# Nine instead of seven up-projection pairs computed as seven half-size products, arranged two and two with one plain pair between

## The chip, the cores and the metric

The kernel runs on one core of one Trainium2 chip. The metric is the device time of one execution in microseconds (us). Engines are named as in the profile: PE is TensorE's matmul and PEld its weight load, DVE is VectorE, ACT is ScalarE, POOL is GpSimd, SP is the SyncE queue that issues most loads. POOL issues its own DMAs.

## The reference

One layer of an encoder: token mixing, cross-attention into a memory, and a gated MLP, each in RMSNorms with a residual. The change touches the MLP's up-projection alone:

```python
def conv_ffn(h, w_up, conv_w, conv_b, w_down):
    u = h @ w_up                       # (512, 1024) @ (1024, 5632)
    ...
    for j in range(CONV_W):
        acc = acc + up[:, j:j + n] * conv_w[j]
    gate, val = jnp.split(acc, 2, axis=-1)
    return (jax.nn.silu(gate) * val) @ w_down
```

There are 512 tokens, a model width of 1024 and 2816 gate and 2816 value columns, all float32.

## The kernel before

**Precision.** A float32 product is made of three matmuls on operands split in a high part and a low part (`mm3`, L278 to L280): high by high, high by low, low by high. A weight arrives as float32 in a tile called `raw` or `tmp` (128x1024, 512 KB) by a DMA that SP issues (L189). ACT casts it to the high part `wh` (L222). The low part `wl` is made in one of two ways: DVE subtracts (L224), or ACT writes the negated high part into `wl` (L229) and a DMA that POOL issues adds the float32 weight from DRAM onto it (L230, an accumulating DMA). Such a `wh`, `wl` pair is called a unit.

**Units ahead.** Units are consumed in one fixed order (`plan`). `take` and `unit` first issue the work on the unit three places further on (`AHEAD = 3`), and the tile pool `wp` has four buffers each of `wh` and `wl`. So unit n goes into the buffers of unit n-4, and its cast can begin only when PE has read unit n-4 for the last time. Four `raw` rooms (two of pool `rawp`, two of pool `t4`) take the loads, and each pair of up-projection units loads into the rooms of the pair two before it.

**The up-projection.** The 5632 columns are taken as 22 pairs i: 128 gate columns and the 128 value columns that belong to them. A plain pair is two units, `w` and `w'`; each is 8 x 3 matmuls with 512 columns (tokens). A pair listed in `UP_S` goes through `strassen_pair` (L1126 on): token halves and weight quarters, seven products in place of eight, each 4 x 3 matmuls with 256 columns, so 84 matmuls of 256 columns in place of 48 of 512. It has four units:

```python
plan += [(kind, UP_S.index(i)) for kind in ("diag", "side", "sums", "last")]
UP_PRODUCTS = (("w11", 0), ("w22", 1), ("t2", 0), ("w21", 1), ("t3", 1), ("t1", 0), ("t4", 0))
LOW_FROM = {"diag": 0, "side": 512}
```

Unit `diag` serves the first two products, `side` the next two, `sums` two, `last` one. `diag` and `side` are loaded; `sums` and `last` are sums of them that DVE makes (`add_blocks`, L197, L200, L204). By `LOW_FROM`, the low part of the whole of `diag` (512 KB) and of the second half of `side` (256 KB) comes by POOL's accumulating DMA; all other units of this stage use DVE's subtraction:

```python
by_dma = 0 if i in NEG_SCALAR or i in NEG_POOL else LOW_FROM.get(kind, raw.shape[1])
nc.scalar.copy(wh, raw)
if by_dma:
    last_low[0] = nc.vector.tensor_sub(wl[:, :by_dma], raw[:, :by_dma], wh[:, :by_dma].bitcast(F32)).ins
if by_dma < raw.shape[1]:
    ...
        nc.scalar.mul(wl[:, by_dma:], wh[:, by_dma:].bitcast(F32), -1.0)
    nc.gpsimd.dma_start(wl[:, by_dma:], source(i)[:, by_dma:], accum_op=ALU.add)
```

After a pair, `conv` (ACT L1067, DVE L1068 and L1070) filters its two results; ACT's Silu (L1073) and DVE's product (L1081) finish it. In `strassen_pair` ACT copies the first product out of PSUM (L1142) and DVE combines the others (L1144 to L1153). A scheduler orders the instructions on each engine.

**Other work of the stage.** The down-projection after it also uses sums of weight blocks. They are made in DRAM by 24 accumulating DMAs of POOL (L251), which are hung on certain units: POOL first copies a mark from that unit's `wl` (L236), so it waits for DVE, and then issues the DMA. `adds_at` lists those units.

Before, pairs 6, 8, 10, 12, 14, 16 and 18 go through `strassen_pair`; between every two of them lies a plain pair. In the profile they begin at 534.0, 555.1, 576.0, 597.0, 618.0, 639.0 and 659.9 us.

Of the kernel before, what the change touches and what calls it, by code (L numbers as in the profile page):

```python
# [25 lines left out]
FF = 2816  # L26
NF = FF // P
EPS = 1e-6
UP_S = (6, 8, 10, 12, 14, 16, 18)
N_MIX, N_WHOLE = 66, 110 - 2 * len(UP_S)  # L30
N_DOWN = N_WHOLE + 4 * len(UP_S)
N_UNITS = N_DOWN + 42
# [57 lines left out]
def layer(tc, io, out):  # L90
# [54 lines left out]
    plan = [("w", i) for i in range(N_MIX)]  # L145
    whole, adds_at = N_MIX, set(ADDS_AT)
    for i in range(NF):
        if i in UP_S:
            plan += [(kind, UP_S.index(i)) for kind in ("diag", "side", "sums", "last")]
        else:  # L150
            if i >= 2:
                adds_at.update((len(plan), len(plan) + (i - 1 not in UP_S)))
            plan += [("w", whole), ("w", whole + 1)]
            whole += 2
    assert len(plan) == N_DOWN and whole == N_WHOLE
# [970 lines left out]
    def strassen_pair(i):  # L1126
        g, m, n = next_bank(), next_bank(), next_bank()
        place = {"w11": (g, near), "t2": (m, far), "t1": (m, near), "w22": (n, near), "t3": (n, far),
                 "w21": (g, near), "t4": (g, far)}
        two, more, val = tmp2(tag="th"), tmp2(tag="th"), tmp2(tag="tq")  # L1130
        for k, (name, at_w) in enumerate(UP_PRODUCTS):
            if k % 2 == 0:
                w = take()
            (hi, lo), cols = left_h[name]
            o, at = place[name]
            o = o[:, at]
            for kc in range(4):
                wc = slice(at_w * 512 + kc * P, at_w * 512 + kc * P + P)
                mm3(o, (w[0][:, wc], w[1][:, wc]), (hi[:, kc, cols], lo[:, kc, cols]), kc == 0 and name != "w21",
                    kc == 3, name == "w21")  # L1140
            if name == "w11":
                nc.scalar.copy(two[:, near], o)  # L1142
            elif name == "t2":
                nc.vector.tensor_sub(two[:, far], o, two[:, near])  # L1144
            elif name == "t3":
                nc.vector.tensor_add(more[:, far], o, two[:, far])
            elif name == "t1":
                nc.vector.tensor_add(more[:, near], o, two[:, far])
                nc.vector.tensor_tensor(out=val.rearrange("p (a t) -> p a t", a=2),
                                        in0=n.rearrange("p (a t) -> p a t", a=2),  # L1150
                                        in1=more[:, None, near].to_broadcast([P, 2, 256]), op=ALU.add)
            elif name == "t4":
                nc.vector.tensor_sub(o, o, more[:, far])  # L1153
        conv(0, i, g)
        conv(1, i, val)

    for i in range(2, NF):
        if i in UP_S:
            strassen_pair(i)
# [185 lines left out]
```

## Time and profile before

| | |
|---|---|
| median of 3 runs | 816.55 us (816.46 to 817.71) |
| profiled execution, its own time | 816.97 us |
| its span, first to last instruction | 814.8 us |
| granted TensorE clock | 0.999 of full speed |
| PE busy | 804.2 us (99%) |
| DVE, ACT, POOL busy | 574.4, 483.6, 137.2 us |

The time lies 2.2 us above the span, for what comes ahead of the first and behind the last instruction. A busy time is the union of an engine's instructions; matmuls overlap one another, so PE's rate is read from the distance between starts and not from the duration of one. A DMA's time is from its issue to its landing.

### The profile page before, as it was taken

How to read it: one execution, taken by the hardware profiler on the slowest of the kernel's cores; microseconds unless marked ns; L12 is line 12 of the kernel's file. 1: busy time of each engine (PE TensorE's matmuls, PEld its weight loads, DVE VectorE, ACT ScalarE, POOL GpSimd, SP SyncE). 2: the span in 40 equal slices, each digit the busy share in tenths (PEclk: the TensorE clock that was granted, in tenths of full speed). 3: DMA queues.
4: the chain of work that ended last, by engine and by line, in shares of the span. 5: the costliest groups of instructions: out<-in, count | busy, mean ns of one | idle time of the engine just before them, and what ended most of it. 6: DMA issues, size and time to landing. Idle time of an engine off the chain costs nothing.

```text
span 814.8 us, 11771 instructions
## 1 busy us (share of the span) xinstructions
PE 804.2 (99%) x4426; PEld 691.4 (85%) x4426; DVE 574.4 (70%) x866; ACT 483.6 (59%) x798; POOL 137.2 (17%) x213
## 2 busy tenths in 40 slices
PE   9999999999999999999999999999999999999996
PEld 7888888889898887888888898899999998888885
DVE  5456587469886875855453767987777788888765
ACT  5675757469988874645553543665555545566651
POOL 0111201053233101301010311211111101000301
PEclk9999999999999999999999999999999999999999
DMA  8585745569889743256734058676666677278852
GB/s 296 197 262 139 160 104 116 119 161 244 230 237 261 186 162 135 78 181 156 181 117 142 27 167 205 154 197 172 177 168 140 162 193 180 90 209 273 243 128 103
DMA packets 42457, 139.61 MB, mean 171 GB/s; under 512 B 5280, under 2 KB 6560, under 8 KB 42400
## 3 DMA queue, kind: packets, MB, share of 16 engines
q1 hardware_dynamic: 28944, 97.43, 35.2%
q0 software_dynamic: 12160, 38.54, 26.3%
q10 hardware_dynamic: 1296, 2.89, 1.0%
q8 instruction: 34, 0.56, 0.3%
q14 instruction: 23, 0.19, 0.1%
HBM read 135.17 MB, written 25.17 MB: 197 GB/s over the span
## 4 chain that ended last, share of the span: by engine, by line
PE 93%; DVE 3%; ACT 1%; POOL 1%; issue 1%; POOLq 0%; DVEq 0%
PE ps_b L279 10%; PE ps_b L278 10%; PE ps_b L280 10%; PE ps_s L280 6%; PE ps_s L279 6%; PE ps_s L278 6%; PE ps_o L278 5%; PE ps_o L279 5%; PE ps_o L280 5%; PE ps_c L280 5%; PE ps_c L279 5%; PE ps_c L278 5%; PE ps_c L646 3%; PE ps_o L891 2%; PE ps_s L870 2%; PE ps_o L880 2%
## 5 line engine op out<-in xcount | busy, mean ns | idle before, releaser
L222 ACT CAST wh<-raw 128x1024 fp32r<-128x1024 f32 x110 | 113.8, 1036 | 114.8 <-PE ps_b L279 35.7
L224 DVE TENSOR_TENSOR wl<-raw,wh 128x1024 fp32r<-128x1024 f32 (+1 forms) x77 | 92.3, 1200 | 72.1 <-ACT wh L222 72.1
L278 PE MATMUL ps_b<-big,wh 128*128 128x512 f32 (+1 forms) x344 | 122.2, 355 | 0.0
L280 PE MATMUL ps_b<-big,wl 128*128 128x512 f32 (+1 forms) x344 | 121.1, 352 | 0.0
L279 PE MATMUL ps_b<-big,wh 128*128 128x512 f32 (+1 forms) x344 | 120.8, 351 | 0.0
L279 PEld LDWEIGHTS ps_b<-big,wh 128*128 128x128 f32 x344 | 65.1, 189 | 8.3
L280 PEld LDWEIGHTS ps_b<-big,wl 128*128 128x128 f32 x344 | 65.0, 189 | 8.3
L278 PEld LDWEIGHTS ps_b<-big,wh 128*128 128x128 f32 x344 | 65.1, 189 | 8.1
L672 DVE TENSOR_TENSOR big<-big 128x512 f32<-128x512 f32 x64 | 47.5, 755 | 10.6 <-PE ps_c L646 4.2
L278 PE MATMUL ps_s<-wh,big 128*128 128x512 f32 (+1 forms) x140 | 53.4, 382 | 0.0
L279 PE MATMUL ps_s<-wl,big 128*128 128x512 f32 (+1 forms) x140 | 53.3, 381 | 0.0
L280 PE MATMUL ps_s<-wh,big 128*128 128x512 f32 (+1 forms) x140 | 52.9, 378 | 0.0
L230 POOL DMA_DIRECT2D wl<-in_w_dram x33 | 29.4, 890 | 127.9 <-ACT wl L229 87.0
L122 DVE TENSOR_TENSOR big<-ps_o,big 128x512 fp32r<-128x512 f32 x54 | 36.9, 687 | 15.1 <-ACT big L121 13.5
L121 ACT CAST big<-ps_o 128x512 fp32r<-128x512 f32 x54 | 31.8, 589 | 18.5 <-PE ps_o L994 7.5
L278 PE MATMUL ps_s<-big,wh 128*128 128x256 f32 (+1 forms) x120 | 40.0, 333 | 0.0
L279 PE MATMUL ps_s<-big,wh 128*128 128x256 f32 (+1 forms) x120 | 39.9, 333 | 0.0
L280 PE MATMUL ps_s<-big,wl 128*128 128x256 f32 (+1 forms) x120 | 39.9, 332 | 0.0
L278 PE MATMUL ps_o<-wh,big 128*128 128x512 f32 (+1 forms) x102 | 39.2, 384 | 0.0
L279 PE MATMUL ps_c<-big,wh 128*128 128x256 f32 (+1 forms) x120 | 39.1, 326 | 0.0
L278 PE MATMUL ps_c<-big,wh 128*128 128x256 f32 (+1 forms) x120 | 39.0, 325 | 0.0
L280 PE MATMUL ps_c<-big,wl 128*128 128x256 f32 (+1 forms) x120 | 39.0, 325 | 0.0
(313 smaller groups left out, 2150.3 us busy)
## 6 DMA issues: line engine op xcount, KB each, us to landing
raw<-in_w_dram SPq DMA_DIRECT2D x91, 512.0 KB, 3.5
wl<-in_w_dram POOLq DMA_DIRECT2D x33, 512.0 KB, 7.1
sum_t<-in_wd_dram SPq DMA_DIRECT2D x20, 512.0 KB, 6.3
tmp<-in_wu_dram SPq DMA_DIRECT2D x14, 512.0 KB, 6.8
sum_t<-in_wd_dram POOLq DMA_DIRECT2D x10, 512.0 KB, 8.2
sum_t<-sum_t POOLq DMA_DIRECT2D x10, 512.0 KB, 7.8
big<-sum_t SPq DMA_DIRECT2D x10, 512.0 KB, 5.1
raw<-sum_t SPq DMA_DIRECT2D x10, 512.0 KB, 3.8
```

The source lines that it names most:

```text
L121: nc.scalar.copy(hi, src)
L122: (eng or nc.vector).tensor_sub(lo, src, hi.bitcast(F32))
L222: nc.scalar.copy(wh, raw)
L224: last_low[0] = nc.vector.tensor_sub(wl[:, :by_dma], raw[:, :by_dma], wh[:, :by_dma].bitcast(F32)).ins
L230: nc.gpsimd.dma_start(wl[:, by_dma:], source(i)[:, by_dma:], accum_op=ALU.add)
L278: nc.tensor.matmul(o, a[0], b[0], start=start, stop=False, skip_group_check=again)
L279: nc.tensor.matmul(o, a[0], b[1], start=False, stop=False, skip_group_check=again)
L280: last_mm[0] = nc.tensor.matmul(o, a[1], b[0], start=False, stop=stop, skip_group_check=again).ins
L646: nc.tensor.matmul(o[:, b, :], kc[:, blk(b)], qc[:, blk(b)] if m == 1 else pat(qk, b * P, [[2 * m, P // (2 * m)], [T + m, 2], [1, m]]), st ...
L672: nc.vector.tensor_tensor(out=c, in0=c, in1=pat(tt, toff + off, [[2, npair], [gap, 2], [0, m]]), op=ALU.mult)
L870: nc.tensor.matmul(s, qT[h // 4][:, h % 4, blk(qb)], kT[:, 2 * (h // 4) + c, :], start=c == 0, stop=c == 1)
L880: nc.tensor.transpose(o[:, c, :], e[:, 0, blk(c)], ident)
```

## The change

Pairs 6, 8, 9, 11, 12, 14, 15, 17 and 18 go through `strassen_pair`; plain pairs in the stage's middle are 7, 10, 13 and 16. So pairs 9, 12, 15 and 18 follow another such pair directly. The second line changes which plain pairs carry one of POOL's additions and which two: now one where both neighbours are in `UP_S` (7, 10, 13, 16), two elsewhere.

```diff
-UP_S = (6, 8, 10, 12, 14, 16, 18)
+UP_S = (6, 8, 9, 11, 12, 14, 15, 17, 18)
...
             if i >= 2:
-                adds_at.update((len(plan), len(plan) + (i - 1 not in UP_S)))
+                adds_at.update((len(plan), len(plan) + (i - 1 not in UP_S or i + 1 not in UP_S)))
```

**ACT, pair 8.** The rows begin with the last filter of pair 7 and the copy of pair 8's first product. In the rows before, the two raw casts are plain pair 9's units and the `tmp` casts pair 10's `diag` and `side`:

```order
L1067 ACTIVATE tmp_5291<-ps_b,cw 128x512
L1142 COPY tmp_5299<-ps_s 128x256
L222 CAST wh<-raw 128x1024 x2
L222 CAST wh<-tmp_5265 128x1024
L229 ACTIVATE wl<-wh 128x1024
L222 CAST wh<-tmp_5306 128x1024
L1067 ACTIVATE tmp_5418<-ps_s,cw 128x512
L1067 ACTIVATE tmp_5423<-tmp_5301,cw 128x512
L229 ACTIVATE wl<-wh 128x512
```

With the change, the raw casts are pair 9's `diag` and `side`, then come its `sums` and `last`:

```order
L1067 ACTIVATE tmp_5289<-ps_b,cw 128x512
L1142 COPY tmp_5297<-ps_s 128x256
L222 CAST wh<-raw 128x1024
L229 ACTIVATE wl<-wh 128x1024
L222 CAST wh<-raw 128x1024
L229 ACTIVATE wl<-wh 128x512
L222 CAST wh<-both 128x1024
L222 CAST wh<-tmp_5370 128x512
L1067 ACTIVATE tmp_5420<-ps_s,cw 128x512
L1067 ACTIVATE tmp_5425<-tmp_5299,cw 128x512
L1142 COPY tmp_5435<-ps_b 128x256
```

The `diag` that is to follow pair 8 directly is cast in the place where a plain unit was cast, which is the first cast after pair 8's start; before, two plain units came ahead of the next `diag`.

**POOL, pairs 8 to 10.** L230 with 128x1024 is a `diag`, with 128x512 the half of a `side`. Before, one such couple is followed by the mark and the addition that hang on a plain unit (plain pair 9):

```order
L230 DMA wl<-in_wu_dram 128x1024
L230 DMA wl<-in_wu_dram 128x512
L236 COPY mark<-wl 128x1
L251 DMA sum_t_3_3028<-sum_t_3_1976 128x1024
L230 DMA wl<-in_wu_dram 128x1024
L230 DMA wl<-in_wu_dram 128x512
```

With the change, two couples (pairs 8 and 9) come behind one another, and the mark (plain pair 10) after both:

```order
L230 DMA wl<-in_wu_dram 128x1024
L230 DMA wl<-in_wu_dram 128x512
L230 DMA wl<-in_wu_dram 128x1024
L230 DMA wl<-in_wu_dram 128x512
L236 COPY mark<-wl 128x1
L251 DMA sum_t_3_3028<-sum_t_3_1976 128x1024
```

Pair 9's two accumulating DMAs have nothing but pair 8's ahead of them in POOL's order.

## Rows read from the trace of the kernel before

**Rows 1.** The page: busy time of each engine, share of the span, instructions.
```profile
PE 804.2 (99%) x4426; PEld 691.4 (85%) x4426; DVE 574.4 (70%) x866; ACT 483.6 (59%) x798; POOL 137.2 (17%) x213
```

**Rows 2.** PE in order of time around pair 16, and where pair 18 begins and ends.
```profile
638.97 0.28 PE L278 MATMUL ps_s<-big,wh 128*128 128x256 f32 x1
...
639.20 0.28 PE L280 MATMUL ps_s<-big,wl 128*128 128x256 f32 x1
...
649.04 0.40 PE L278 MATMUL ps_b<-big,wh 128*128 128x512 f32 x1
...
659.94 0.28 PE L278 MATMUL ps_c<-big,wh 128*128 128x256 f32 x1
...
670.02 0.40 PE L278 MATMUL ps_s<-big,wh 128*128 128x512 f32 x1
```

**Rows 3.** Windows: pairs 16 and 17, pair 17 alone, pair 16 alone (length, engines, clock, DMA).
```profile
638.97:659.94 20.97, 20.97 (x133) 19.08 (x132) 16.17 (x23) 11.71 (x16) 2.75 (x4) 1.00 0.66 164
649.04:659.94 10.90, 10.90 (x50) 9.01 (x49) 8.58 (x13) 6.68 (x10) 1.73 (x2) 1.00 0.93 233
638.97:649.04 10.07, 10.07 (x86) 10.07 (x85) 7.59 (x11) 5.02 (x7) 1.02 (x2) 1.00 0.36 88
```

**Rows 4.** ACT in order of time during pairs 16 and 17 (start, duration, what).
```profile
641.92 1.05 ACT L222 CAST wh<-raw 128x1024 fp32r<-128x1024 f32 x1 [0.95 <-PE ps_o L279]
644.80 1.05 ACT L222 CAST wh<-raw 128x1024 fp32r<-128x1024 f32 x1 [1.83 <-PE ps_s L279]
647.68 1.05 ACT L222 CAST wh<-tmp 128x1024 fp32r<-128x1024 f32 x1 [1.83 <-PE ps_c L279]
648.80 1.06 ACT L229 ACTIVATE wl<-wh 128x1024 fp32r<-128x1024 f32 x1
...
652.09 0.62 ACT L229 ACTIVATE wl<-wh 128x512 fp32r<-128x512 f32 x1
```

**Rows 5.** POOL in order of time: the issues of pair 18's two accumulating DMAs.
```profile
650.16 0.88 POOL L230 DMA_DIRECT2D wl<-in_wu_dram  x1 [4.54 <-ACT wl L229]
653.00 0.85 POOL L230 DMA_DIRECT2D wl<-in_wu_dram  x1 [1.96 <-ACT wl L229]
```

**Rows 6.** DMA issues in windows at 650.0, 545.0 and 653.0 us: size, time to landing.
```profile
wl<-in_wu_dram POOLq DMA_DIRECT2D x1, 512.0 KB, 8.9
...
wl<-in_wu_dram POOLq DMA_DIRECT2D x1, 512.0 KB, 9.8
...
wl<-in_wu_dram POOLq DMA_DIRECT2D x1, 256.0 KB, 8.0
```

**Rows 7.** PE and POOL in order of time, DMA issue at 531.0 us: pair 6's `side`.
```profile
538.55 0.36 PE L280 MATMUL ps_b<-big,wl 128*128 128x256 f32 x1
538.75 0.28 PE L278 MATMUL ps_b<-big,wh 128*128 128x256 f32 x1
...
531.10 0.88 POOL L230 DMA_DIRECT2D wl<-in_wu_dram  x1 [4.34 <-ACT wl L229]
...
wl<-in_wu_dram POOLq DMA_DIRECT2D x1, 256.0 KB, 7.4
```

**Rows 8.** Mixing stage: SP and POOL issues; DMA at 71.5, 156.5, 164.0 us.
```profile
70.61 0.33 SPq L189 DMA_DIRECT2D raw<-in_w_dram  x1
...
71.97 0.87 POOL L230 DMA_DIRECT2D wl<-in_w_dram  x1 [9.86 <-PE ps_s L280]
...
wl<-in_w_dram POOLq DMA_DIRECT2D x1, 512.0 KB, 5.3
...
wl<-in_w_dram POOLq DMA_DIRECT2D x1, 512.0 KB, 5.2
...
wl<-in_w_dram POOLq DMA_DIRECT2D x1, 512.0 KB, 5.6
```

**Rows 9.** DMA issue at 193.0 us, with two transfers issued within 1.8 us ahead.
```profile
wl<-in_w_dram POOLq DMA_DIRECT2D x1, 512.0 KB, 6.1
```

**Rows 10.** DVE in order of time: the subtraction for one plain unit in this stage.
```profile
622.02 1.23 DVE L224 TENSOR_TENSOR wl<-raw,wh 128x1024 fp32r<-128x1024 f32 x1 [0.46 <-ACT wh L222]
```

## The prediction

> **What bounds the kernel now.** I read the page first. PE is busy 99% of the span [rows 1]. So time is gained only where PE gets less to do, and anything that makes PE wait is lost in full. Then PE in order of time in the stage that changes [rows 2]: pair 16 begins at 638.97 us, pair 17 at 649.04, pair 18 at 659.94 and pair 19 at 670.02. A pair in seven products takes 10.07 or 10.08 us, a plain one 10.90. The windows over the same stretches [rows 3] show PE without a gap, at the full one of its two clock levels (1.00, 2.4 GHz). They show one thing more: DMA is busy 36% while pair 16 runs and 93% while pair 17 runs. The reader is to keep that in mind, since the change moves a DMA from the full stretch into the empty one, but also brings its deadline nearer.
>
> **What PE saves.** Two plain pairs (9 and 15; 11 and 17 take the places of 10 and 16) become pairs in seven products. Each saves 10.90 - 10.08 = 0.82 us, together 1.64 us. Nothing else in this stage can be gained, as PE has no gaps there to close. 0.2% of 816.55 us is 1.63 us, about what a measurement of this kernel can tell from no change, so even the whole gain would barely be seen.
>
> **What the change makes late.** The first unit of a pair in seven products (`diag`) gets its low part by ACT's cast, ACT's negated copy and an accumulating DMA from POOL. It is issued three units ahead into the buffers of the unit four places before it.
>
> Before, those are the buffers of the preceding such pair's `sums`, with a plain pair still to come. The cast of pair 18's `diag` starts at 647.68 us and the copy at 648.80 [rows 4]; POOL issues at 650.16 [rows 5], 2.48 us after the cast began. The DMA takes 8.9 us [rows 6], so it lands at 659.0 or 659.1. Pair 18 begins at 659.94: about one microsecond to spare. Another such DMA, for pair 8, took 9.8 us [rows 6].
>
> With the change, the `diag` of pairs 9, 12, 15 and 18 follows such a pair directly, and unit n-4 is that pair's own `diag`. Its buffers are read until the second product ends, 24 matmuls after the start. A cast with exactly this release is in the trace: the one at 641.92 us, 2.95 us after pair 16's start [rows 2, 4]. Adding the 2.48 us, POOL issues at 2.95 + 2.48 = 5.43 us after the first pair's start. POOL has nothing else to do before it.
>
> The deadline: the first matmul that reads `wl` is the third of the next pair, 10.07 + 0.23 = 10.30 us after the first pair's start (0.23 is 639.20 - 638.97 [rows 2]). How late a landing may be is seen at pair 6's `side`: issued at 531.10 and 7.4 us under way, it landed at 538.5 us; the matmul after the one at 538.55 came 0.20 us later where the usual step is 0.12 [rows 7]. So PE resumed some 0.13 us after the landing (538.55 + 0.08 - 538.50), and the landing must come by 10.17. That leaves 10.17 - 5.43 = **4.74 us** for the DMA. Whatever it takes beyond that stops PE, four times.
>
> **How long the DMA takes there.** This is the term that decides.
> - In the full stretch it took 8.9 and 9.8 us [rows 6]. That is the upper end.
> - The nearest pattern is in the mixing stage, where a plain unit's low part goes the same way [rows 8]: a 512 KB load is issued at 70.61, as soon as a cast frees its room, and the accumulating DMA at 71.97, 1.36 us later. It took 5.3 us; two others with that lead took 5.2 and 5.6. 5.2 is the lower end. With two transfers issued shortly ahead it took 6.1 [rows 9].
> - In the changed place the cast ends 2.95 + 1.05 = 4.00 us after the first pair's start and frees the room for one load (pair 11's `diag`, in the case of pair 9), 1.4 us ahead of the DMA, as in rows 8. The next load must wait for the `side` cast, which starts at 5.83 us (644.80 - 638.97 [rows 2, 4]), and a DVE subtraction after it; it comes some 2.2 us behind the DMA, too late to slow much of it. The addition in DRAM that hangs on a plain unit (L251) is long done or not yet issued.
>
> I take 5.6 us, the largest of rows 8, since something does run behind its tail. The stall is 5.6 - 4.74 = 0.86 us, four times 3.44 us. **Sum:** 3.44 - 1.64 = +1.80 us. On the profiled execution's own 816.97 us that is 818.8; the median of the runs is 0.42 lower, so 818.4 us.
>
> The Trainium skill, "DMA: Bandwidth & Descriptors", section "Anatomy of one DMA — SWDGE (gpsimd) path", fits such a DMA as 2.0 us plus its bytes at 436 GB/s. For 512 KB that is an estimate of 3.2 us, within 4.74: no stall, and 814.9 us. The trace does not agree: the least of rows 8 is 5.2 us.
>
> **What costs nothing, and under which cover.**
> - The `side` half (256 KB): cast at 5.83, copy and issue as in rows 4 and 5 (1.12 + 0.91), so issued at 7.86. Its deadline is 2.88 us (24 steps of 0.12) after `diag`'s, and moves with the stall: 10.17 + 0.86 + 2.88 = 13.91. That leaves 6.05 us for half the bytes of a transfer that I take at 5.6, so I cost it at nothing. In the full stretch it took 8.0 us [rows 6]: the other bound, a rival below.
> - DVE: a pair in seven products and a plain one together need 16.17 us of DVE [rows 3]; the plain one has two subtractions of 1.23 us [rows 10]. Two such pairs and a plain one so need at most 2 x 16.17 - 2 x 1.23 = 29.9 us of about 31.0. ACT needs 11.71 of 20.97 [rows 3] and has more room. If DVE fell behind, the product t1 of such a pair would be late next, since it waits for DVE to have read its PSUM bank.
> - POOL's additions: 24 as before, some on later units. Each waits for DVE through its mark, and what is queued behind it is the next `diag`, not due for several microseconds. The sums are read in the down-projection, after 700 us.
> - SP: as many loads of the same size.
>
> **Rivals.**
> 1. *Covered (faster).* The DMA lands within 4.74 us or is issued sooner; PE never waits. 816.55 - 1.64 = 814.9 us. For it: the stretch is the emptiest of the stage (36% [rows 3]). Against it: it would have to beat every 512 KB row shown by 0.5 us. It decides as soon as the DMA needs under 4.74 us.
> 2. *`side` is late too (slower).* If its half takes 7.0 us, between 6.05 and the 8.0 of rows 6, PE waits another 0.95 us, four times 3.8: 822.2 us. For it: it queues behind `diag`'s transfer and beside the second load.
> 3. *The full stretch follows the DMA (slower).* More transfers in flight than I count, and it takes 8.9 us as before: stall 4.16, four times 16.6, 831.6 us. At 7.4 us it is +9.0 and 825.6. The skill's same page, section "Queues, rings and completion order", says that the DMA engines take turns between the queues, packet by packet. By that rule a load beside it would stretch it; rows 6 against rows 8 agree, with 8.9 against 5.3 us.
> 4. *Seven products are not what they seem*, or the saving is eaten elsewhere to the same amount: no change, 816.6 us. The order on PE shows the 256-column matmuls for all nine pairs, which speaks against it.
>
> **How the numbers follow.** Chances: my forecast with 5.2 to 6.1 us (816.8 to 820.4 us, by the same sum) 0.52; rival 1 0.06; rival 2 0.18; rival 3 0.16; rival 4 0.08. The time is that of the forecast, 818.4. The range leaves out rival 1 and the upper half of rival 3: from 816.2, a little under the forecast's own lower end and rival 4, to 826.0, where the DMA takes 7.4 to 7.5 us. Slower by over 0.2% begins at a stall of 0.82 us, which is a DMA of 5.56 us. So the forecast's 0.52 divides about evenly: 0.27 slower, 0.25 the same. With rivals 2 and 3 slower gets 0.27 + 0.18 + 0.16 = 0.61; with rival 4 the same gets 0.33; faster has rival 1 alone, 0.06.
>
> **What the profile after would show.** Right: PE has four gaps of near 0.9 us, at the third matmul of pairs 9, 12, 15 and 18, ended by a POOL DMA; that DMA is issued 5.4 us after the preceding pair's start and takes 5 to 6 us; each pair in seven products takes 10.08 us but for the gap; plain pairs keep 10.9. Wrong: no gap there (rival 1), a second gap twelve matmuls and more later, at `side` (rival 2), gaps of several microseconds (rival 3), or a wait of PE for DVE or ACT, which nothing above allows for.

## The result and the profile after

The changed kernel takes 820.17 us (median of 6 runs, 819.70 to 821.17), the kernel before 816.88 us beside it (6 runs, 816.46 to 817.78): ratio 1.0041, 95% interval 1.0031 to 1.0051, so 3.3 us slower. The profiled execution took 820.6 us, its span is 818.8 us; before, 816.97 and 814.8.

The whole of PE's waiting from 480 us on, by the view of waits (who waited for whom: us in total, times, longest), is one row, with four waits; before, that view had no row for PE there:

```profile
PE ps_b L280 <- DMA wl<-in_wu_dram: 3.8, 4, 1.2
```

PE in order of time at the start of pairs 9 and 12 answers to [rows 2]. The third matmul, the first that reads `wl`, starts 1.00 and 1.42 us after the second, where a step is 0.12:

```profile
565.55 0.28 PE L279 MATMUL ps_b<-big,wh 128*128 128x256 f32 x1
566.55 0.39 PE L280 MATMUL ps_b<-big,wl 128*128 128x256 f32 x1 [0.72 <-DMA wl<-in_wu_dram]
566.78 0.28 PE L278 MATMUL ps_b<-big,wh 128*128 128x256 f32 x1
...
597.59 0.28 PE L279 MATMUL ps_b<-big,wh 128*128 128x256 f32 x1
599.01 0.39 PE L280 MATMUL ps_b<-big,wl 128*128 128x256 f32 x1 [1.14 <-DMA wl<-in_wu_dram]
```

Windows over the four couples (8 and 9, 11 and 12, 14 and 15, 17 and 18) and over plain pair 10, as in [rows 3] (length, busy time of PE, PEld, DVE, ACT, POOL, clock, DMA share, GB/s):

```profile
555.36:576.49 21.13, 20.41 (x169) 20.20 (x168) 17.59 (x27) 12.62 (x17) 3.03 (x4) 1.00 0.51 123
576.49:587.40 10.91, 10.91 (x51) 9.02 (x49) 8.63 (x13) 6.81 (x10) 2.84 (x4) 1.00 1.01 250
...
587.40:608.95 21.55, 20.41 (x169) 20.20 (x168) 17.59 (x27) 12.74 (x17) 3.07 (x4) 1.00 0.57 146
619.86:641.44 21.58, 20.41 (x170) 20.21 (x168) 17.59 (x27) 12.75 (x17) 3.02 (x4) 1.00 0.57 126
652.35:673.50 21.15, 20.41 (x170) 20.21 (x168) 17.59 (x27) 12.52 (x16) 3.98 (x6) 1.00 0.52 122
```

Two pairs of 10.07 us would be 20.14. The couples are 0.99, 1.41, 1.44 and 1.01 us above that, together 4.85 us. (The view of waits has 3.8: it counts from the end of the matmul before, which lasts 0.28 us, while the next would have started after 0.12.) Less the 1.64 us that the two more pairs save, that is 3.2 us of the 3.6 by which the profiled executions differ. The rest is small: nearly 0.2 us in the first product of the down-projection, and 0.14 us at pair 6's `side` (that pair takes 10.28 us, before 10.14).

The DMAs that PE waited for (issue on ACT's and POOL's timelines, then size and time to landing for the couples in the same order), against [rows 4 to 6]:

```profile
559.39 1.06 ACT L229 ACTIVATE wl<-wh 128x1024 fp32r<-128x1024 f32 x1
...
560.75 0.85 POOL L230 DMA_DIRECT2D wl<-in_wu_dram  x1 [11.48 <-ACT wl L229]
...
591.43 1.06 ACT L229 ACTIVATE wl<-wh 128x1024 fp32r<-128x1024 f32 x1
...
593.50 0.89 POOL L230 DMA_DIRECT2D wl<-in_wu_dram  x1 [12.19 <-ACT wl L229]
...
wl<-in_wu_dram POOLq DMA_DIRECT2D x1, 512.0 KB, 5.8
...
wl<-in_wu_dram POOLq DMA_DIRECT2D x1, 512.0 KB, 5.5
...
wl<-in_wu_dram POOLq DMA_DIRECT2D x1, 512.0 KB, 6.2
...
wl<-in_wu_dram POOLq DMA_DIRECT2D x1, 512.0 KB, 5.8
```

Pair 9's DMA is issued 560.75 - 555.36 = 5.39 us after pair 8 began and lands at 566.5; PE goes on. Pair 12's took only 5.5 us but was issued 6.10 us after pair 11 began: 1.01 us passed from the end of ACT's copy to the issue, where 0.30 is usual. The kernel before shows the same 1.01 us once, at pair 10's `side` (copy done at 589.77, issue at 590.78), where it cost nothing; so such a lateness is there without the change too, and its cause is open.

### The profile page after: what moved, and what is told of

Read it like the earlier page. It is cut to its first block, busy times and chain, and to the rows that moved or that the text cites. A ratio compares the mean times of both kernels' runs of the same rounds, so it can differ in the third digit from the quotient of the medians.

```text
span 818.8 us, 11963 instructions
## 1 busy us (share of the span) xinstructions
PE 803.2 (98%) x4498; PEld 693.3 (85%) x4498; DVE 582.5 (71%) x884; ACT 491.2 (60%) x808; POOL 141.0 (17%) x217
## 4 chain that ended last, share of the span: by engine, by line
PE 78%; DMA 8%; issue 6%; DVE 4%; ACT 2%; POOL 1%; SPq 0%; POOLq 0%; DVEq 0%; ACTq 0%
PE ps_b L280 9%; PE ps_b L278 9%; PE ps_b L279 9%; DMA wl<-in_wu_dram 7%; PE ps_s L279 5%; PE ps_s L278 5%; PE ps_s L280 5%; PE ps_o L278 4%; PE ps_o L280 4%; PE ps_o L279 4%; PE ps_c L278 3%; PE ps_c L279 3%; PE ps_c L280 3%; PE ps_c L646 3%; PE ps_o L891 2%
## 5 line engine op out<-in xcount | busy, mean ns | idle before, releaser
L280 PE MATMUL ps_b<-big,wl 128*128 128x512 f32 (+1 forms) x364 | 128.2, 352 | 3.8 <-DMA wl<-in_wu_dram 3.8
L224 DVE TENSOR_TENSOR wl<-raw,wh 128x1024 fp32r<-128x1024 f32 (+1 forms) x73 | 85.2, 1170 | 64.4 <-ACT wh L222 63.6
L278 PE MATMUL ps_b<-big,wh 128*128 128x512 f32 (+1 forms) x364 | 128.9, 354 | 0.0
L279 PE MATMUL ps_b<-big,wh 128*128 128x512 f32 (+1 forms) x364 | 127.5, 350 | 0.0
L280 PEld LDWEIGHTS ps_b<-big,wl 128*128 128x128 f32 x364 | 68.8, 189 | 13.3 <-DMA wl<-in_wu_dram 4.8
L279 PEld LDWEIGHTS ps_b<-big,wh 128*128 128x128 f32 x364 | 68.9, 189 | 8.6
L278 PEld LDWEIGHTS ps_b<-big,wh 128*128 128x128 f32 x364 | 68.9, 189 | 8.4
L230 POOL DMA_DIRECT2D wl<-in_w_dram x33 | 29.3, 887 | 127.2 <-ACT wl L229 86.3
L229 ACT ACTIVATE wl<-wh 128x1024 fp32r<-128x1024 f32 (+1 forms) x42 | 40.7, 968 | 1.0
L278 PE MATMUL ps_s<-big,wh 128*128 128x256 f32 (+1 forms) x128 | 38.9, 304 | 0.0
L279 PE MATMUL ps_s<-big,wh 128*128 128x256 f32 (+1 forms) x128 | 38.8, 303 | 0.0
L278 PE MATMUL ps_o<-big,wh 128*128 128x512 f32 (+1 forms) x112 | 38.7, 345 | 0.0
L279 PE MATMUL ps_o<-big,wh 128*128 128x512 f32 (+1 forms) x112 | 38.6, 345 | 0.0
```

What stands on the lines that cost most here:

```text
L278: nc.tensor.matmul(o, a[0], b[0], start=start, stop=False, skip_group_check=again)
L279: nc.tensor.matmul(o, a[0], b[1], start=False, stop=False, skip_group_check=again)
L280: last_mm[0] = nc.tensor.matmul(o, a[1], b[0], start=False, stop=stop, skip_group_check=again).ins
```

## The experiments

The theory after the result: each couple loses what the accumulating DMA for the second pair's `diag` is late by, because its buffers come free late. The rivals: DVE is too heavily loaded, or nine such pairs are too much for the DMA engines. Each run is compared with the kernel before, measured beside it. Line numbers of the runs' rows are shifted by the lines added.

### One part undone: only one couple

```diff
-UP_S = (6, 8, 9, 11, 12, 14, 15, 17, 18)
+UP_S = (6, 8, 9, 11, 13, 15, 17)
```

> Edit: pairs 6, 8, 9, 11, 13, 15 and 17 in seven products: seven, as in the kernel before, with one couple of neighbours. Theory: one gap of 0.9 to 1.4 us at the third matmul of pair 9, nothing else moves: about 816.9 + 1.2 = 818.1 us. Rival (the loss comes from having nine of them in the stage, not from the neighbourhood): no change, 816.9 us.

818.00 us against 817.03 (ratio 1.0012, interval 1.0003 to 1.0020). PE has one wait from pair 8 on:

```profile
PE ps_b L280 <- DMA wl<-in_wu_dram: 0.5, 1, 0.5
```

The couple took 20.93 us, 0.79 above 20.14; seven pairs in all, as before. So the loss goes with the neighbourhood and not with the number; here it was somewhat under what was expected. The other 0.2 us of the run is a longer wait at pair 6's `side` (10.32 us for the pair, before 10.14).

### Diag's low part by DVE

```diff
         by_dma = 0 if i in NEG_SCALAR or i in NEG_POOL else LOW_FROM.get(kind, raw.shape[1])
+        if kind == "diag" and UP_S[plan[i][1]] - 1 in UP_S:
+            by_dma = raw.shape[1]
```

> Edit: the low part of diag in pairs 9, 12, 15 and 18 is made by DVE's subtraction, as for a plain unit, in place of ACT's negated copy and POOL's accumulating DMA. Theory (the four gaps of PE are the landing of that DMA, 0.9 to 1.3 us each): all four gaps go, 4.4 us, so about 820.2 - 4.8 = 815.4 us, a little under the kernel before. Rival (nine such pairs load DVE too much, and any work added to it comes out as PE waiting for DVE; four more subtractions are 4.9 us of DVE): the gaps stay or turn into waits for DVE, 819 to 821 us.

819.04 us against 817.03 (1.0022, 1.0014 to 1.0031): 2.0 us are lost where it was 3.3, so somewhat over a third is back. The time is in the rival's range, but neither side's reason was right: PE still waits for a DMA, and another one. The waits, then POOL's issue of pair 9's `side` and PE's wait there:

```profile
PE ps_b L282 <- DMA wl<-in_wu_dram: 3.2, 4, 1.8
...
564.21 0.86 POOL L232 DMA_DIRECT2D wl<-in_wu_dram  x1 [15.50 <-DVE wl L226]
...
569.97 0.39 PE L282 MATMUL ps_b<-big,wl 128*128 128x256 f32 x1 [0.39 <-DMA wl<-in_wu_dram]
```

PE no longer waits at pair 9's third matmul but at the 39th, the third of the product that reads the second half of `side`, which the DMA makes. That DMA was issued at 563.20 us in the changed kernel, 7.84 after pair 8's start, and here at 564.21, 9.42 after it (554.79): by the row, POOL waits until DVE has written the other half of the same `wl`, and DVE now comes to that later, with `diag`'s subtraction ahead. So something like rival 2 of the prediction stands right behind the first cause, and DVE's added work counts after all, by way of POOL's issue.

### Half of diag's low part by DVE

```diff
+        if kind == "diag" and UP_S[plan[i][1]] - 1 in UP_S:
+            by_dma = 512
```

> Edit: only the first half of that diag's low part by DVE; the second half (256 KB) still by copy and DMA. Theory: the first product reads the first half alone, so no wait at the third matmul; the second half is due 12 steps of 0.12 us, 1.44 us, later, that is 6.2 us after an unchanged issue, and the 512 KB took 5.5 to 6.2 us: no gaps, about 815.4 us. Rival (what counts is when POOL's DMA of this pair lands, whatever it carries, since PE's wait is one for the whole tile): gaps of 0.5 to 1.3 us stay at the third matmul, 818 to 820 us.

817.79 us against 817.03 (1.0016, 1.0005 to 1.0026). No wait at the third or the 15th matmul: the 256 KB for the second half took 4.7 us for pair 9 and landed in time. The four waits that are left are at `side` (below, pair 9's two DMAs):

```profile
PE ps_b L282 <- DMA wl<-in_wu_dram: 1.2, 4, 0.4
...
wl<-in_wu_dram POOLq DMA_DIRECT2D x1, 256.0 KB, 4.7
...
wl<-in_wu_dram POOLq DMA_DIRECT2D x1, 256.0 KB, 6.1
```

The rival's idea, one wait for the whole tile, is not decided here: the DMA was issued at 559.88 and landed at 564.6, before pair 9's first matmul even (564.99). The 2.4 us that the theory fell short by are `side`: the couples took 20.67, 20.78, 20.60 and 20.78 us, together 2.27 above four times 20.14. Its DMA was issued at 563.80 for pair 9 and took 6.1 us.

### The same bytes in two DMAs

```diff
+                if kind == "diag" and UP_S[plan[i][1]] - 1 in UP_S:
+                    for c in range(2):
+                        nc.scalar.mul(wl[:, half(c)], wh[:, half(c)].bitcast(F32), -1.0)
+                        nc.gpsimd.dma_start(wl[:, half(c)], source(i)[:, half(c)], accum_op=ALU.add)
...
```

> Edit: that diag's low part still all by copy and DMA, but in two halves, each with its own copy and its own DMA of 256 KB; nothing is added to DVE. Theory: the first DMA is issued some 0.4 us sooner and carries half, so it lands 0.4 to 1.5 us sooner than the 512 KB did: gaps of at most 0.5 us, 815.4 to 817 us. Rival (a DMA's time here is nearly all fixed, and the second one is later): gaps of 0.5 to 0.9 us at the first or second product, 817.5 to 819.5 us.

822.58 us against 817.03 (1.0064, 1.0043 to 1.0084). Its six runs lie between 818.4 and 824.4 us, so no gain on the changed kernel is seen, and a loss is likely. The first DMA took 5.0 to 5.2 us and was in time or nearly; the second, issued some 0.55 us behind it, took 6.4 to 8.1 us. In the profiled execution (821.4 us) PE's waits moved from the first product to the second, in three couples of four. Of pair 12, the third and the 15th matmul are shown too:

```profile
PE ps_c L286 <- DMA wl<-in_wu_dram: 4.0, 3, 1.7
...
597.17 0.28 PE L286 MATMUL ps_b<-big,wl 128*128 128x256 f32 x1
...
599.99 0.39 PE L286 MATMUL ps_c<-big,wl 128*128 128x256 f32 x1 [1.22 <-DMA wl<-in_wu_dram]
```

The third matmul, which reads the first half, went ahead at 597.17 while the DMA for the second half of the same tile was still under way. So PE does not wait for the whole tile, and the rival's idea in the run before falls here. The same bytes in two DMAs bring nothing; the second half alone, in the run before, took 4.2 to 4.7 us, so what helped there is likely that fewer bytes were in flight.

### An earlier cast: a tile of its own for the second diag

Eight pairs (18 is plain); the second `diag` of each couple does not wait for the first's buffers.

```diff
-UP_S = (6, 8, 9, 11, 12, 14, 15, 17, 18)
+UP_S = (6, 8, 9, 11, 12, 14, 15, 17)
...
+        if kind == "diag" and UP_S[plan[i][1]] - 1 in UP_S:
+            own = big([P, 2, 1024], F32R)
+            wh, wl = own[:, 0], own[:, 1]
...
```

> Edit: pairs 6, 8, 9, 11, 12, 14, 15 and 17 (eight, three couples), and the diag of the second of each couple has a tile of its own for its high and low part, so that its cast need not wait for the preceding diag's buffers; copy and DMA are as they were. Theory (the early deadline is that of the buffer): the DMA is issued well before 5.4 us after the first pair's start, no gap at pairs 9, 12 and 15, 817.0 - 0.8 = 816.2 us. Rival (the DMA takes what it takes, and issued earlier it collides with the first pair's own): gaps at pairs 9, 12, 15 or at 8, 11, 14, 818 us or more.

818.87 us against 816.92 (1.0027, 1.0018 to 1.0036). The couples 11, 12 and 14, 15 took 20.15 us each, no gap: that part of the theory holds, the late buffer made the DMA late. But at the first couple POOL issued pair 9's DMA ahead of pair 8's, and PE waited at pair 8 itself, where the rival had a gap. The rival's reason, two DMAs that collide, is not what the rows show: pair 8's took 9.2 us, no more than before [rows 6], but it was issued 6.28 us before the pair began, in the changed kernel 9.78 (545.58 for 555.36). ACT had cast pair 9's `diag` first, once its load had come, and pair 8's behind it. POOL's two issues, PE, and the granted clock in windows after it:

```profile
547.65 0.88 POOL L234 DMA_DIRECT2D big<-in_wu_dram  x1 [6.26 <-ACT big L233]
548.60 0.85 POOL L234 DMA_DIRECT2D wl<-in_wu_dram  x1
...
557.83 0.39 PE L284 MATMUL ps_s<-big,wl 128*128 128x256 f32 x1 [2.56 <-DMA wl<-in_wu_dram]
...
555.00:558.00 3.00, 0.44 (x4) 0.24 (x3) 1.74 (x3) 1.82 (x3) 0.00 (x0) 1.00 0.96 234
558.00:561.00 3.00, 3.00 (x20) 3.00 (x21) 3.00 (x6) 0.37 (x1) 0.00 (x0) 0.72 0.44 95
561.00:564.00 3.00, 3.00 (x21) 3.00 (x21) 0.89 (x3) 1.68 (x2) 0.44 (x1) 0.71 0.41 156
564.00:567.00 3.00, 3.00 (x28) 3.00 (x27) 1.70 (x3) 1.05 (x1) 0.41 (x1) 1.00 0.68 124
```

The couple took 24.45 us, 4.3 too long: 2.7 by the wait, and some 1.5 because PE then ran at the lower of its two clock levels for part of six microseconds. Both sides were half right. (The profiled execution took 820.13 us, 1.3 more than the median, so the loss at this couple is likely smaller in others.)

### Nine pairs without neighbours

```diff
-UP_S = (6, 8, 9, 11, 12, 14, 15, 17, 18)
+UP_S = (4, 6, 8, 10, 12, 14, 16, 18, 20)
...
-                adds_at.update((len(plan), len(plan) + (i - 1 not in UP_S or i + 1 not in UP_S)))
+                adds_at.update((len(plan), len(plan) + 1))
```

> Edit: nine pairs in seven products without neighbours, pairs 4, 6, 8 and so on to 20, with POOL's additions two on each plain pair. Theory (the loss comes from the neighbourhood alone): no gap at the third matmul of any of the nine, 817.0 - 1.6 = 815.4 us, if pairs 4 and 20 bring no wait of their own at the stage's two ends. Rival (nine such pairs are too much for DMA or DVE): gaps at every one of them, 818 us or more.

831.74 us against 816.92 (1.0179, 1.0165 to 1.0193). PE waited at pairs 6, 8, 10, 14 and 16 for a `diag` DMA of 10.7 to 10.9 us, 0.7 to 1.3 us each, at pair 4 for the sums of h (1.5 us for ACT, 2.4 for DVE; the granted clock then fell to 0.50 for some microseconds), and 1.6 us for DVE at the start of the down-projection. The theory's time was far off, but this does not decide the question, since the run also put two additions on each plain pair. The next run separates that.

### Two additions on each plain pair, nothing else

```diff
-                adds_at.update((len(plan), len(plan) + (i - 1 not in UP_S)))
+                adds_at.update((len(plan), len(plan) + 1))
```

This is an edit of the kernel before, with its seven pairs.

> Edit: the seven pairs of the kernel before (6, 8 and so on to 18), but POOL's additions in DRAM two on each plain pair, as in the run with pairs 4 to 20; nothing else. Theory (there the diag of a lone pair landed late because a second addition runs into its DMA, and not because there are nine pairs): the DMA takes 10 to 11 us where it took 8.7 to 9.9, so it lands 0.5 to 1 us too late at four or five of the six lone pairs behind a plain one: 817 + 4 = 821 us. Rival (the additions are harmless, the ninth pair is what loads the stage): no gaps, 817 us.

822.09 us against 816.78 (1.0067, 1.0052 to 1.0083). PE waited at the `diag` of pairs 8, 12 and 14 and at pair 6's `side`; at pair 8 the addition's DMA and the `diag` DMA after it took

```profile
sum_t<-sum_t POOLq DMA_DIRECT2D x1, 512.0 KB, 11.0
...
wl<-in_wu_dram POOLq DMA_DIRECT2D x1, 512.0 KB, 12.4
```

against 8.9 to 9.8 for a `diag` before [rows 6]. So a second addition on the plain pairs is enough to make `diag` late, at three lone pairs where four or five were expected. These are the pairs whose second addition moves 512 KB too (`diag` took 10.4 to 12.4 us); at pairs 10 and 16 it moves 256 KB, `diag` took 9.8 and 9.6, and there is no gap. For the changed kernel this suggests that its rule, one addition where both neighbours are in seven products, kept the first pairs of the couples free of gaps; no run with its nine pairs and two additions there shows it.

### No early DMA left

Two ways. By the first, `diag` and `side` of pairs 9, 12, 15 and 18 are wholly DVE's; by the second, only the second half of their `diag` is left to a DMA:

```diff
+        if kind in LOW_FROM and UP_S[plan[i][1]] - 1 in UP_S:
+            by_dma = raw.shape[1]
```

```diff
+        if kind in LOW_FROM and UP_S[plan[i][1]] - 1 in UP_S:
+            by_dma = {"diag": 512, "side": 1024}[kind]
```

> Edit: in pairs 9, 12, 15 and 18 the low parts of diag and of side are both made by DVE's subtraction; no accumulating DMA is left in these four pairs. Theory (with diag's DMA gone, PE waited 0.5 to 2.0 us for side's DMA, the next one with the same early deadline): no gap of PE is left at these four pairs, 817.0 - 1.6 = 815.4 us, at most 816 with 0.2 to 0.5 us lost elsewhere. Rival (DVE is at its limit, with 1.9 us more per couple than in the changed kernel): PE waits for DVE in these pairs, 817 us or more.

> Edit: as half_low (diag's first half by DVE, its second half by DMA), and side wholly by DVE: one DMA of 256 KB is left in each of the four pairs, due 1.44 us later than diag's first half. Theory: half_low's four gaps (0.35 to 0.55 us each at side) go, and the DMA left took 4.1 to 4.7 us of some 6.2: 817.8 - 1.8 = 816.0 us, no gap. Rival (DVE): waits for DVE, 817 us or more.

816.03 us against 816.92 (0.9989, 0.9980 to 0.9997) and 816.50 (0.9990, 0.9981 to 0.9999). With DVE alone, couples 8, 9 and 17, 18 took 20.15 us, twice 10.07; with the half DMA three of the four took 20.18 to 20.20. What waits are left, 0.5 and 0.2 us by the view of waits, are at the first pair of a couple (11 and 14; 11), whose `diag` is still a full DMA. The forecasts were 815.4 and 816.0 us with no gap, so both runs gained somewhat less. No wait for DVE appears. The rival of the overloaded DVE falls, for an arrangement of two such pairs in three.

### A version that beats both

From the second of these, `diag`'s first half by DVE in every such pair, with nine pairs, and then with ten:

```diff
-LOW_FROM = {"diag": 0, "side": 512}
+LOW_FROM = {"diag": 512, "side": 512}
...
-UP_S = (6, 8, 9, 11, 12, 14, 15, 17, 18)
+UP_S = (6, 8, 9, 10, 12, 13, 14, 16, 17, 18)
```

Both keep the lines by which `side` of a pair behind another such pair is wholly DVE's. The second has an `or i == 11` in the rule of the additions besides, so that all of them find a unit.

> Edit: as half_side, and in the five other pairs too (6, 8, 11, 14, 17) diag's first half is made by DVE, the second half by DMA. Theory (a diag due 1.44 us later and half as large is never late; half_side kept 0.34 us at pair 11): no gap at any of the nine pairs, 816.5 - 0.4 = 816.1 us or less. Rival (0.6 us more of DVE per couple is too much): waits for DVE, 816.5 us or more.

> Edit: low parts as in half_all, and ten pairs in seven products: 6, then 8 to 10, 12 to 14, 16 to 18, so three in a row. Theory (the neighbourhood is harmless once no early DMA is left): 0.82 us less than half_all, 815.3 us, 1.6 us under the kernel before. Rival (DVE: by the windows of before such a row with its plain pair needs some 39 us of DVE in 41 us): waits for DVE or ACT at the third of each row, 816.5 us or more.

Nine pairs: 815.39 us against 816.78 (0.9985, 0.9976 to 0.9994). Ten: 814.43 (0.9971, 0.9962 to 0.9979), 2.4 us under the kernel before, where the change was 3.3 above it. The view of waits has no row for PE from 480 us on in either. Of the ten, windows over pairs 8 to 10 and over plain pair 11:

```profile
555.09:585.35 30.26, 30.26 (x253) 30.26 (x252) 28.17 (x42) 17.97 (x24) 3.86 (x6) 1.00 0.44 112
585.35:596.26 10.91, 10.91 (x50) 9.02 (x49) 10.86 (x17) 5.77 (x9) 2.82 (x4) 1.00 1.03 256
sum 41.17, PE 41.17 PEld 39.28 DVE 39.03 ACT 23.74 POOL 6.68; mean PE 20.59 PEld 19.64 DVE 19.52 ACT 11.87 POOL 3.34
```

DVE is at 39.03 of 41.17 us, 95% and the figure expected, and still PE does not wait. An eleventh pair would have little DVE left to use; it was not tried.

## Why the prediction was right, and where its sum was short

- **What bounds, and what PE saves:** right. PE had no gap before but for 0.07 us at pair 6's `side`, and pairs and plain pairs keep 10.07 and 10.91 us. So rival 4 falls: the saving is there, under the waits.
- **The mechanism and its place:** right, at all four pairs and at the third matmul. The experiments show its parts: with one couple there is one gap, with `diag`'s DMA gone the gap at the third matmul is gone, and with a buffer of its own it is gone at all three couples, at the price of one at pair 8.
- **The allowance of 4.74 us:** right for pair 9: 5.8 us of DMA would give a stall of 5.8 - 4.74 - 0.04 (issue at 5.39 for 5.43) = 1.02; measured 0.99, within the rounding of the 5.8.
- **The term that was mis-sized:** "The stall is 5.6 - 4.74 = 0.86 us, four times 3.44 us." Measured 4.85. In three couples the DMA took 5.8, 6.2 and 5.8 us, more than any of rows 8: two of them within the edge of 6.1 that rows 9 gave, one just over it. The size was off, not the mechanism. What made these DMAs longer than rows 8 is open: the prediction's "something does run behind its tail" does not account for it, since at pair 12 the next load and `side`'s DMA came sooner behind it than at the others (1.54 and 1.75 us, for 2.25 and 2.45), and its DMA was the shortest. The load ahead of it had a longer start there (2.07 us, for 1.36), which no run separates. That DMA took 5.5 us, but POOL issued it 0.7 us late; why is open too. The sum so came to +3.2 us in place of +1.8, and the runs say +3.3.
- **The range and the chances:** slower was to begin at a DMA of 5.56 us, and it took more than that in three of four. The 820.17 us lie at the upper edge of the forecast's own 816.8 to 820.4.
- **`side` at nothing:** right for the changed kernel by luck, as two errors cancelled. The DMA was given 6.05 us and took 6.8, so by the prediction's own figures `side` would have been 0.75 us late. But the deadline was wrong too. "Its deadline is 2.88 us (24 steps of 0.12) after `diag`'s" is the deadline of the half that DVE makes; the half that the DMA makes is first read 36 steps after, by the 39th matmul, 570.97 us at pair 9 (rows 7 have that matmul: 538.55 is 4.55 us after pair 6's start). The DMA landed at 570.0 (563.20 + 6.8): 0.97 us to spare after a stall of 0.99, so without the stall nothing would have been left. It took 6.8 us for half of `diag`'s bytes, longer than `diag`'s own DMA. As soon as `diag` was mended by DVE alone it was next, as rival 2 described, and that is why the mend by DVE for `diag` alone brought so little.
- **DVE:** right. The bound was 29.9 us per couple and plain pair, and 26.22 (17.59 + 8.63) were needed. That t1 would be late next was never tested: in no run of this arrangement did PE wait for DVE.
- **Rival 1** did not come: the DMA took 5.5 to 6.2 us, and under 4.74 was needed. By the fit in the Trainium skill, "DMA: Bandwidth & Descriptors", "Anatomy of one DMA — SWDGE (gpsimd) path", 512 KB would have taken an estimated 3.2 us, with no stall and 814.9 us. The trace decides against it, for these DMAs that add onto what is there.
- **Rival 3** did not come: the first `diag` of each couple, in the full stretch, still took 8.6 to 9.2 us, the second did not.

## What to carry to other kernels

Before putting two costly steps next to each other, go back from each of their inputs to what frees its buffer. Here the plain pair between two such pairs fell away, the time from `diag`'s cast to its first use shrank from 12 us to 7, and a transfer that had been hidden set the pace. A mend must take away the next deadline too, or the wait only moves: DVE for `diag` alone gave somewhat over a third back, for `diag` and `side` all of it. And where PE is full, work on another engine can be free even at 95% of its time, as DVE's was here, if nothing it makes is due early.

## What the runs showed of the hardware

- Accumulating DMAs in this stage, with few others in flight: 256 KB took 4.1 to 4.3 us at the second pair of each couple in the run with nine pairs and half DMAs, 512 KB 5.5 to 6.2 us in the changed kernel. The same 512 KB with two additions ahead took 9.6 to 12.4 us on seven pairs.
- After PE had stood for 2.56 us, its granted clock was 0.72 and 0.71 in the next two windows of 3 us, part of them at the lower of its two levels with matmuls 0.21 us apart where 0.12 is usual, and 1.00 after that. With two additions on each plain pair PE stood for 2.23 us at pair 8, and the clock was 0.70 and 0.68 in the next two windows (2.5 and 3 us). In the run with DVE's `diag`, where PE stood for at most 1.8 us, the clock stayed at 1.00. The two longer waits so cost more than their length.
- Two DMAs of half the size, some 0.55 us behind one another: the second took 6.4 to 8.1 us from its issue, where one of the whole took 5.5 to 6.2.
- The first product of the down-projection lost nearly 0.2 us in every run with the change's nine pairs. Of the others only the run with pairs 4 to 20 lost time there, by its wait for DVE. The cause was not followed.
